# A hybrid two-layer trunk in fp32: one block of tokens runs ahead of the other between the layers, and layer B begins with two V products

## The chip, the cores and the metric

The kernel runs on one core of one Trainium2 chip. The core has a matrix engine (TensorE, "PE" in the profile; its weight loads are listed apart as "PEld"), a vector engine (VectorE, "DVE"), a scalar engine (ScalarE, "ACT"), GpSimd ("POOL") and a sync engine whose queue ("SP") issues the DMAs here. Weights and inputs are in HBM; tiles of 128 partitions are in SBUF; matmuls write into PSUM. The metric is the time of one execution on the device in microseconds, lower is better.

## The reference, cut to what matters

One sequence of 256 tokens, width 2048, goes through two layers: A (a Mamba-2 mixer) and B (dilated attention with shared K and V). Each layer ends with a residual, a gate and a LayerNorm over the 2048 features of a token.

```
def reference(x, c, ada_w, ada_b, ln_g, ln_b, a_in_w, ..., a_out_w, kv_w, b_in_w, b_out_w):
    for layer in range(2):
        shift, scale, gate = _adaln(c, ada_w[layer], ada_b[layer])     # silu(c) @ w + b
        h = x * (1.0 + scale) + shift
        if layer == 0:
            y = _ssd_mixer(h, ...)            # ends with y(256 x 4096) @ out_w(4096 x 2048)
        else:
            y = _dilated_mixer(h, k_sh, v_sh, b_in_w[0], b_out_w[0])
        x = _layer_norm(ALPHA * x + (1.0 + gate) * y, ln_g[layer], ln_b[layer])
        if layer == 0:
            k_sh, v_sh = split(x @ kv_w)      # kv_w: 2048 x 6144, K is the first half, V the second
    return x
```

K and V have three groups (g) of eight heads of 128 features. The kernel works on half a group at a time: `hq` is 0 or 1, and a half group is 512 columns.

## The kernel before, in words

**Tiling.** The 256 tokens are two blocks of 128 (`b` = 0, 1), the 2048 features sixteen tiles of 128 (`kt`). All matmuls are fp32 with split operands: every weight piece (128x1024 f32, 512 KB) is loaded by the SP queue into one of six `raw` buffers (`load_piece`, L85), ScalarE makes its rounded high half `whi` (L93), VectorE the low half `wlo` = raw - whi (L95). There are four buffers of each half. A product then has three matmuls per tile: high x high, high x low, low x high.

**Three forms of product.** `tm_mults` (L166) has the tokens as the stationary operand, 512 weight columns move, and the result is token-major; one piece (q) covers two feature tiles and has 6 matmuls for each block (L172 to L174). `cm_piece` (L109) has weights as the stationary operand and 256 tokens move; the result is feature-major (L119 to L121). `cm_wide` (L140) does the same for 256 columns with a 512-wide matmul over the high and low half of the tokens at once (L151) and a 256-wide one (L152), and adds the two sums (L156, L157). `tm_chunk` (L179) runs a whole token-major product; its last `split_end` pieces are held back, so that block 0's matmuls of them come first and then block 1's.

**Background work.** `queue` and `background` (L100, L253) spread the dot products of the next layer's scales, shifts and gates (L237, a 1 MB load and a 2048-wide VectorE operation each) over the pieces; `rate` (a, b) means a jobs per b pieces.

**The seam between the layers.** Layer A's output product is four `tm_chunk` calls over 512 columns (n = 0 to 3, L669), each followed for each block by `residual` (L648: gate, residual, statistics `bn_stats`). After the fourth, `ln_scale` (L654) makes mean and inverse deviation of both blocks in one chain of small VectorE operations, then u is normalised in five column ranges, block 0 on ScalarE (L687), block 1 on VectorE (L689). `x_tiles` (L698) transposes u into feature-major tiles on PE (L702), scales them into the high half `xhi` on ScalarE (L705), again in full precision into `xtmp` on VectorE (L706), and takes the difference as the low half `xlo` (L707). Layer B's first work is the three K products of hq = 0, whose pieces alternate (`cm_quads`, L123), with the x tiles of the next q made ahead of each. Behind them come the K products of hq = 1 (`cm_wide`), then the six V products (`tm_chunk`), with background jobs at a rate of (4, 9). While these run, GpSimd turns u into the residual of layer B (L759, L760).

**Order.** Each engine executes its instructions in order. The framework sets that order by the program's order as a priority and by what it takes to be ready; `tc.issue_after(ins)` puts the instructions of a block behind `ins` on its engine. Before, the low halves of the first weight pieces and all that follows the K products is put behind `nb_last`, the last operation of `ln_scale`.

**Memory.** Layer A's outputs y (eight tiles of 4 KB a partition) are in the pool `pa`, which is closed at the seam; the pool `pb` holds K and V in four tiles of 12 KB (`kk0`, `kk1`, `vt0`, `vt1`), two of them reused for the split gated output `oghi`, `oglo`, two for held weights of the last product.

Of the kernel before, what the change touches and what calls it, by code (L numbers as in the profile page):

```python
# [9 lines left out]
F32 = mybir.dt.float32  # L10
F32R = mybir.dt.float32r
# [12 lines left out]
G = 8  # L24
# [25 lines left out]
def trunk(ctx, tc, xT, x, c, par, cst, bias, lnrow, ada, wdt, win, wout, wkv, wk1, wbin, wbout, out):  # L50
# [72 lines left out]
    def cm_quads(work, ahi, alo, pre=None, after=None):  # L123
        for q in range(KT // 2):
            if pre:
                pre(q)
            for src, ps in work:
                cm_piece(src, q, ps, ahi, alo, after=after if q == 0 else None)

# [69 lines left out]
    sm.tile([P, 8], F32, name="pad", bufs=1)  # L199
# [72 lines left out]

    with ExitStack() as cA:
        pa = cA.enter_context(tc.tile_pool(name="pa", bufs=1))

        y = [pa.tile([P, 2, 512], F32, name=f"y{g}") for g in range(G)]
# [377 lines left out]
        def ln_scale(blocks=(0, 1)):  # L654
# [3 lines left out]
            for i, b in enumerate(blocks):  # L658
# [22 lines left out]
        drain()  # L681
        r, nb, nb_last = ln_scale()
        for c0_, c1_ in ((0, 256), (256, 512), (512, 1024), (1024, 1536), (1536, 2048)):
            for b in range(2):
                cs_ = slice(c0_, c1_)
                if b == 0:
                    S.activation(u[b][:, cs_], u[b][:, cs_], AF.Identity, bias=nb[:, b:b + 1], scale=r[:, b:b + 1])  # L687
                else:
                    V.tensor_scalar(u[b][:, cs_], u[b][:, cs_], r[:, b:b + 1], nb[:, b:b + 1],  # L689
                                    op0=ALU.mult, op1=ALU.add)  # L690
# [7 lines left out]
    def x_tiles(q):  # L698
        for kt in (2 * q, 2 * q + 1):
            pt = aux.tile([P, 512], F32, name="aux")[:, :L]  # L700
            for b in range(2):
                T.transpose(pt[:, b * P:b * P + P], u[b][:, kt * P:kt * P + P], ident)  # L702
            t = pl.tile([P, L], F32, name="xtmp")
            g_, b_ = pv("lng")[:, kt:kt + 1], pv("lnb")[:, kt:kt + 1]
            S.activation(xhi[:, kt, :], pt, AF.Identity, bias=b_, scale=g_)  # L705
            V.tensor_scalar(t, pt, g_, b_, op0=ALU.mult, op1=ALU.add)  # L706
            V.tensor_tensor(xlo[:, kt, :], t, xhi[:, kt, :].bitcast(F32), op=ALU.subtract)  # L707

    def ahead(q):

        if q == 0:
            x_tiles(0)
        if q < KT // 2 - 1:
            x_tiles(q + 1)

    kk = [pb.tile([P, 12, L], F32, name=f"kk{i}").rearrange("p (g i) l -> p g i l", g=NG) for i in range(2)]
    vt = [pb.tile([P, NG, 2, 512], F32, name=f"vt{i}") for i in range(2)]

    def evict_k(hq, g, ps):
        for w in range(2):  # L720
            S.activation(kk[hq][:, g, 2 * w:2 * w + 2, :], ps[w], AF.Copy)

    with ExitStack() as cL:
        pl = cL.enter_context(tc.tile_pool(name="pl", bufs=3))
        ex = cL.enter_context(tc.tile_pool(name="ex1", bufs=2, space=PSUM))
# [234 lines left out]
```

## Time and profile before

| what | value |
|---|---|
| median of three runs | 1301.03 us (1299.05 to 1304.12) |
| the profiled execution | 1303.79 us, span 1302.0 us |
| mean granted TensorE clock in it | 0.988 |
| HBM read | 332.41 MB |
| K products of hq = 0 (L119 first and last start) | 745.6 to 820.1 us |
| K products of hq = 1 (L151 first and last start) | 820.5 to 888.0 us |

How to read it: the span is the time from the first to the last instruction of the profiled execution, and its own time is a little longer. Busy times are sums over an engine's instructions; matmuls are pipelined, so the distance between starts, not the duration of one, is what a matmul costs in a stream. In the rows by stage, each engine has its busy time and the number of its instructions, then come the TensorE clock granted (1.00 is full), the mean busy share of the 16 DMA engines, and GB/s. The chain of waits is followed back from the last instruction; each line is start, time and what ran.

### The profile page before, as it was taken

What the parts mean: (1) busy time and instruction counts of PE and PEld (TensorE: products, weight loads), DVE (VectorE), ACT (ScalarE), POOL (GpSimd) and SP (SyncE); (2) the same over time, 40 slices, a digit from 0 to 9 for tenths busy, and PEclk for the clock granted to TensorE, in tenths of its full rate; (3) what the DMA queues carried; (4) which work ended last, traced back from release to release, by engine and by line L of the source; (5) the groups of instructions that cost most, each with busy time, mean ns of one, the idle gap of its engine ahead of it and who ended that gap; (6) DMA issues with size and microseconds to landing.
All of it is one profiled execution on the core that took longest, in us unless ns stands there. A gap on an engine that the chain in (4) does not pass through costs nothing.

```text
span 1302.0 us, 19326 instructions
## 1 busy us (share of the span) xinstructions
PE 1244.2 (96%) x7378; PEld 1096.7 (84%) x7378; DVE 1028.6 (79%) x1457; ACT 709.6 (55%) x1036; POOL 26.6 (2%) x20
## 2 busy tenths in 40 slices
PE   4999999999999999999999799999999999999995
PEld 3878988899898999878888699888887888888884
DVE  6689887899998778899775577988777757758677
ACT  3544457867587686864333444444435645444651
POOL 0000000000000000000000043000000000000000
PEclk9999999999999999999999899999999999999998
DMA  9999967696884556389977575999897864353561
GB/s 381 421 367 419 382 205 249 221 345 243 288 312 152 187 180 209 117 324 331 383 262 218 190 244 163 354 376 367 329 344 268 274 192 146 106 189 95 162 259 65
DMA packets 80445, 335.86 MB, mean 258 GB/s; under 512 B 8960, under 2 KB 9056, under 8 KB 67552
## 3 DMA queue, kind: packets, MB, share of 16 engines
q1 hardware_dynamic: 80352, 334.62, 71.7%
q8 instruction: 58, 0.95, 0.3%
q14 instruction: 35, 0.29, 0.1%
HBM read 332.41 MB, written 2.18 MB: 257 GB/s over the span
## 4 chain that ended last, share of the span: by engine, by line
PE 82%; DVE 9%; DMA 4%; ACT 3%; issue 2%; SPq 0%; DVEq 0%; ACTq 0%
PE acc L151 13%; PE acc L173 12%; PE acc L174 11%; PE acc L172 11%; PE acc L121 8%; PE acc L120 8%; PE acc L119 8%; PE acc L152 6%; DMA araw<-in_ada 4%; DVE araw L237 2%; DVE wlo L95 2%; PE py L579 1%; PE aux L788 1%; ACT whi L93 1%; DVE cacc L306 1%
## 5 line engine op out<-in xcount | busy, mean ns | idle before, releaser
L95 DVE TENSOR_TENSOR wlo<-raw,whi 128x1024 fp32r<-128x1024 f32 x395 | 484.9, 1240 | 191.4 <-ACT whi L93 189.9
L93 ACT ACTIVATE whi<-raw 128x1024 fp32r<-128x1024 f32 x395 | 412.8, 1056 | 334.8 <-PE acc L174 140.8
L119 PE MATMUL acc<-actT,whi 128*128 128x256 f32 x960 | 274.1, 288 | 23.4 <-ACT whi L93 19.3
L173 PE MATMUL acc<-wlo,actT 128*128 128x512 f32 x704 | 277.2, 394 | 3.2 <-DVE wlo L95 3.1
L121 PE MATMUL acc<-actT,wlo 128*128 128x256 f32 x960 | 272.3, 288 | 4.5 <-DVE wlo L95 4.4
L120 PE MATMUL acc<-actT,whi 128*128 128x256 f32 x960 | 273.8, 286 | 0.6 <-DVE actT L384 0.6
L172 PE MATMUL acc<-whi,actT 128*128 128x512 f32 x704 | 272.9, 395 | 0.8 <-ACT actT L634 0.7
L151 PE MATMUL acc<-actT,whi 128*128 128x512 f32 x704 | 250.9, 398 | 0.0
L237 DVE SCALAR_TENSOR_TENSOR araw<-araw,cb__72 128x2048 f32<-128x2048 f32 x96 | 219.4, 2286 | 17.0 <-DMA araw<-in_ada 16.5
L119 PEld LDWEIGHTS acc<-actT,whi 128*128 128x128 f32 x960 | 186.8, 196 | 25.3 <-ACT whi L93 20.4
L152 PE MATMUL acc<-actT,wlo 128*128 128x256 f32 x704 | 201.4, 286 | 0.0
L121 PEld LDWEIGHTS acc<-actT,wlo 128*128 128x128 f32 x960 | 185.9, 195 | 7.1 <-DVE wlo L95 7.0
L120 PEld LDWEIGHTS acc<-actT,whi 128*128 128x128 f32 x960 | 187.7, 196 | 1.0 <-DVE actT L384 0.8
L174 PE MATMUL acc<-whi,actT 128*128 128x512 f32 x448 | 175.5, 392 | 0.0
L173 PEld LDWEIGHTS acc<-wlo,actT 128*128 128x128 f32 x704 | 132.7, 188 | 33.4 <-DVE wlo L95 6.9
L151 PEld LDWEIGHTS acc<-actT,whi 128*128 128x128 f32 x704 | 132.3, 188 | 30.2
L172 PEld LDWEIGHTS acc<-whi,actT 128*128 128x128 f32 x704 | 132.2, 188 | 28.7 <-ACT actT L634 1.5
L152 PEld LDWEIGHTS acc<-actT,wlo 128*128 128x128 f32 x704 | 133.2, 189 | 0.5
L174 PE MATMUL acc<-whi,ylo 128*128 128x512 f32 x256 | 100.3, 393 | 0.0
L174 PEld LDWEIGHTS acc<-whi,actT 128*128 128x128 f32 x448 | 84.4, 188 | 17.2
L174 PEld LDWEIGHTS acc<-whi,ylo 128*128 128x128 f32 x256 | 48.0, 188 | 9.7
L306 DVE SCALAR_TENSOR_TENSOR cacc<-acc,prm,cacc 128x253 f32<-128x253 f32 (+2 forms) x96 | 42.0, 474 | 6.6 <-ACT cacc L303 6.4
(204 smaller groups left out, 1077.8 us busy)
## 6 DMA issues: line engine op xcount, KB each, us to landing
araw<-in_ada SPq DMA_DIRECT2D x96, 1024.0 KB, 7.4
raw<-in_win SPq DMA_DIRECT2D x160, 512.0 KB, 5.4
raw<-in_wkv SPq DMA_DIRECT2D x72, 512.0 KB, 6.1
raw<-in_wout SPq DMA_DIRECT2D x64, 512.0 KB, 5.2
raw<-in_wbin SPq DMA_DIRECT2D x64, 512.0 KB, 3.6
raw<-in_wk SPq DMA_DIRECT2D x24, 512.0 KB, 7.8
cbc<-cumd SPq DMA_DIRECT2D x16, 512.0 KB, 5.2
raw<-in_wbout SPq DMA_DIRECT2D x16, 512.0 KB, 3.7
```

The lines of the kernel that those rows point to most:

```text
L93: S.activation(hi, raw, AF.Copy)
L95: latest[0] = V.tensor_tensor(lo, raw, hi.bitcast(F32), op=ALU.subtract)
L119: T.matmul(o, hi[:, k, c_], ahi[:, kt, :], start=first, stop=False, skip_group_check=True)
L120: T.matmul(o, hi[:, k, c_], alo[:, kt, :], start=False, stop=False, skip_group_check=True)
L121: T.matmul(o, lo[:, k, c_], ahi[:, kt, :], start=False, stop=kt == k1 - 1, skip_group_check=True)
L151: T.matmul(ps[n], hi[:, k, c_], xp[:, kt], start=kt == 0, stop=False, skip_group_check=True)
L152: T.matmul(ps[n][:, 0, :], lo[:, k, c_], xhi[:, kt, :], start=False, stop=kt == KT - 1, skip_group_check=True)
L172: T.matmul(ps[b], h_, hi[:, k, :], start=kt == k0, stop=False)
L173: T.matmul(ps[b], h_, lo[:, k, :], start=False, stop=False)
L174: T.matmul(ps[b], l_, hi[:, k, :], start=False, stop=kt == k1 - 1)
L237: V.scalar_tensor_tensor(raw, raw, 1.0, cb_, op0=ALU.mult, op1=ALU.mult, accum_out=mod[layer][:, ct, j:j + 1])
L306: V.scalar_tensor_tensor(acc[:, o:], ps[:, :L - o], w[:, j:j + 1], acc[:, o:], op0=ALU.mult, op1=ALU.add)
```

## The change: block 0 goes ahead, and V comes first

- The last product of layer A's output holds four pieces back instead of two. After it, each block has its own residual, its own `ln_scale((b,))` and its own normalisation of the first 512 columns; the rest is normalised later.
- During that product (q = 2, 5, 8, 11) the first four weight pieces of two V products (q = 0 and 1 of `wv[0]` and `wv[2]`) are loaded and split, into tiles that held y (`first_weights`). y now lies in a pool `slots` that stays open; its eight tiles then hold weights, K and V, the gated output and held weights.
- Layer B begins with these two V products. For each block: four x tiles of that block alone, the rest of its normalisation, then the matmuls of the four early pieces for that block; x tiles 4 and 5 come in the middle of block 1's. Then q = 2 to 7 alternate between the two products, with two x tiles ahead of each q.
- Behind them: the third V product of hq = 0, all six K half groups by `cm_wide`, the three V products of hq = 1. The form with weights stationary and 256 tokens moving (`cm_quads`) is no longer used here.
- The splits of q = 2 and all that follows the first two products are put behind `tile4`, the last operation of block 1's fourth x tile.
- The background jobs of layer A's products have rate (1, 2) in the second and third product and are drained after the third.

```diff
-    sm.tile([P, 8], F32, name="pad", bufs=1)
+    sm.tile([P, 16], F32, name="pad", bufs=1)
...
+    slots = ctx.enter_context(tc.tile_pool(name="slots", bufs=1))
...
-        y = [pa.tile([P, 2, 512], F32, name=f"y{g}") for g in range(G)]
+        y = [slots.tile([P, 2, 512], F32, name=f"s{g}") for g in range(G)]
...
+        first_v, norm = [], []
+
+        def normalise(b, c0_, c1_):
+            (r, nb, _), cs_ = norm[b], slice(c0_, c1_)
+            if b == 0:
+                S.activation(u[b][:, cs_], u[b][:, cs_], AF.Identity, bias=nb, scale=r)
+            else:
+                V.tensor_scalar(u[b][:, cs_], u[b][:, cs_], r, nb, op0=ALU.mult, op1=ALU.add)
+
+        def first_weights(q):
+
+            if q % 3 == 2 and q < 12:
+                i = q // 3
+                into = [slots.tile([P, 1024], F32R, name=f"s{2 * i + j}") for j in range(2)]
+                first_v.append(split(load_piece(wv[2 * (i % 2)][i // 2]), into=into))
+
         for n in range(4):
             ps = tm_chunk(wout[n], lambda kt: yhi[kt // 16][:, kt % 16, :], lambda kt: ylo[kt // 4][:, kt % 4, :],
-                          nk=2 * KT, rate=(1, 3) if n else (0, 1), pre=None if n else y_ahead,
-                          split_end=2 if n == 3 else 0)
+                          nk=2 * KT, rate=(1, 2) if n in (1, 2) else (0, 1),
+                          pre={0: y_ahead, 3: first_weights}.get(n), split_end=4 if n == 3 else 0)
             if n == 0:
                 queue(pn, cols1[:16])
+            if n == 2:
+                drain()
...
                 residual(n, ps[b], b, (gt, u[b][:, 512 * n:512 * n + 512]), xr)
-        drain()
-        r, nb, nb_last = ln_scale()
-        for c0_, c1_ in ((0, 256), (256, 512), (512, 1024), (1024, 1536), (1536, 2048)):
-            for b in range(2):
...
+                if n == 3:
+                    norm.append(ln_scale((b,)))
+                    normalise(b, 0, 256)
+                    normalise(b, 256, 512)
...
+    def x_tile(kt, blocks=(0, 1)):
+        c_ = slice(P * blocks[0], P * blocks[-1] + P)
+        pt = aux.tile([P, 512], F32, name="aux")[:, :L]
+        for b in blocks:
+            T.transpose(pt[:, b * P:b * P + P], u[b][:, kt * P:kt * P + P], ident)
+        t = pl.tile([P, L], F32, name="xtmp")
+        g_, b_ = pv("lng")[:, kt:kt + 1], pv("lnb")[:, kt:kt + 1]
+        S.activation(xhi[:, kt, c_], pt[:, c_], AF.Identity, bias=b_, scale=g_)
+        V.tensor_scalar(t[:, c_], pt[:, c_], g_, b_, op0=ALU.mult, op1=ALU.add)
+        return V.tensor_tensor(xlo[:, kt, c_], t[:, c_], xhi[:, kt, c_].bitcast(F32), op=ALU.subtract)
...
-        ps = [acc_pair(), acc_pair(), acc_pair(ex)]
-        cm_quads([(wkv[2 * g], ps[g]) for g in range(NG)], xhi, xlo, pre=ahead, after=nb_last.ins)
-        for g in range(NG):
-            evict_k(0, g, ps[g])
+
+        vps = [tm_pair(), tm_pair()]
+        for b in range(2):
+            for kt in range(4):
+                tile4 = x_tile(kt, (b,))
+            for n in range(1, 4):
+                normalise(b, 512 * n, 512 * n + 512)
+            for i, w in enumerate(first_v):
+                if b and i == 2:
+                    x_tile(4)
+                    x_tile(5)
+                tm_mults(i // 2, w, vps[i % 2], hx, lx, 0, KT, (b,))
+        for q in range(2, KT // 2):
+            if q < KT // 2 - 1:
+                x_tile(2 * q + 2)
+                x_tile(2 * q + 3)
+            for j in range(2):
+                w = split(load_piece(wv[2 * j][q]), after=tile4.ins if q == 2 else None)
+                tm_mults(q, w, vps[j], hx, lx, 0, KT, range(2))
+        for g in range(2):
+            evict_v(0, g, vps[g])
 
         R = (4, 9)
         pin[0] = latest[0].ins
-        with tc.issue_after(nb_last.ins):
+        with tc.issue_after(tile4.ins):
             queue(pl, cols1[16:])
             jobs.append(lambda: gate_out(1))
-            for g in range(NG):
-                for w in range(2):
-                    cm_wide(wk1[2 * g + w], kk[1][:, g, 2 * w:2 * w + 2, :], rate=R)
+            evict_v(0, 2, tm_chunk(wv[4], hx, lx, rate=R))
             for hq in range(2):
                 for g in range(NG):
-                    ps = tm_chunk(wkv[6 + 2 * g + hq], hx, lx, rate=R)
-                    for b in range(2):
-                        S.activation(vt[hq][:, g, b, :], ps[b], AF.Copy)
+                    kv[hq, g] = place(3 + 3 * hq + g, [P, 4, L])
+                    for w in range(2):
+                        cm_wide(wk[2 * (2 * g + hq) + w], kv[hq, g][:, 2 * w:2 * w + 2, :], rate=R)
+            for g in range(NG):
+                evict_v(1, g, tm_chunk(wv[1 + 2 * g], hx, lx, rate=R))
             drain()
...
-    oghi = pb.tile([P, H, L], F32R, name="kk0")
-    oglo = pb.tile([P, H, L], F32R, name="vt0")
...
+    oghi, oglo = ([slots.tile([P, 4, L], F32R, name=f"s{2 * hq + i}") for hq in range(2)] for i in range(2))
...
-    spare = {"hi": pb.tile([P, 3, 1024], F32R, name="kk1"), "lo": pb.tile([P, 3, 1024], F32R, name="vt1")}
     held = []
     for i in range(8):
-        into = [spare[h][:, i, :] if i < 3 else pf.tile([P, 1024], F32R, name=f"{h}{i}") for h in ("hi", "lo")] \
-            if i < 7 else None
+        j = 4 + 2 * i
+        into = [slots.tile([P, 1024], F32R, name=f"s{j + k}") if j < 8 else
+                pb.tile([P, 1024], F32R, name=f"b{j + k}") if j < 12 else
+                pf.tile([P, 1024], F32R, name=f"f{j + k}") for k in range(2)] if i < 7 else None
         held.append(split(load_piece(wbout[2 + i // 4][i % 4]), into=into))
```

Here `place(i, shape)` gives the tile `s{i}` of `slots` for i under 8 and `b{i}` of `pb` above, and `evict_v(hq, g, ps)` copies the two blocks of a V product from PSUM into its place with ScalarE (places 0 to 2 for hq = 0, 9 to 11 for hq = 1).

More of the change, by code (lines that the diff above doesn't have):

```diff
@@ L696, in trunk @@
     hx, lx = (lambda kt: xhi[:, kt, :]), (lambda kt: xlo[:, kt, :])
-    def x_tiles(q):
-        for kt in (2 * q, 2 * q + 1):
-            pt = aux.tile([P, 512], F32, name="aux")[:, :L]
-            for b in range(2):
[L702 to L707, printed above, removed]
@@ L723, in trunk, with place, evict_v @@
+    kv, vt = {}, {}
+    def place(i, shape):
+        return slots.tile(shape, F32, name=f"s{i}") if i < 8 else pb.tile(shape, F32, name=f"b{i}")
+    def evict_v(hq, g, ps):
+        vt[hq, g] = place(3 * hq + g if hq == 0 else 9 + g, [P, 2, 512])
+        for b in range(2):
+            S.activation(vt[hq, g][:, b, :], ps[b], AF.Copy)
     with ExitStack() as cL:
         pl = cL.enter_context(tc.tile_pool(name="pl", bufs=3))
-        ex = cL.enter_context(tc.tile_pool(name="ex1", bufs=2, space=PSUM))
@@ L726, in trunk @@
[L726 to L729 removed]
+        vps = [tm_pair(), tm_pair()]
+        for b in range(2):
+            for kt in range(4):
[7 more added lines that the diff above has]
+                tm_mults(i // 2, w, vps[i % 2], hx, lx, 0, KT, (b,))
@@ L787, in attend @@
                     pq = aux.tile([P, 512], F32, name="aux")[:, :n]
-                    T.matmul(pq, qq[:, g, i, b * P:b * P + P], kk[hq][:, g, i, :n], start=True, stop=True)
+                    T.matmul(pq, qq[:, g, i, b * P:b * P + P], kv[hq, g][:, i, :n], start=True, stop=True)
                     bi = pc2.tile([P, 256], F32, name="bi", bufs=2)[:, :n]
```

39 lines of the change are left out of this document (7 added, 32 removed).

## The prediction

> **What bounds the kernel now.** The page first: who is busy, and which engine the chain of waits runs through.
>
> ```profile
> span 1302.0 us, 19326 instructions
> PE 1244.2 (96%) x7378; PEld 1096.7 (84%) x7378; DVE 1028.6 (79%) x1457; ACT 709.6 (55%) x1036; POOL 26.6 (2%) x20
> PE 82%; DVE 9%; DMA 4%; ACT 3%; issue 2%; SPq 0%; DVEq 0%; ACTq 0%
> ```
>
> TensorE (PE) is the bound, so a change can pay in three ways: fewer or cheaper matmuls, less idle PE, or less time at a lowered clock. Next the busy times by stage: two of the four products of layer A's output (the second and the fourth), then the seam between the layers in three pieces.
>
> ```profile
> core 0: us, PE busy (x) PEld busy (x) DVE busy (x) ACT busy (x) POOL busy (x), PEclk, DMA share, GB/s
> ...
> 606.00:649.50 43.50, 43.50 (x194) 36.02 (x193) 35.49 (x36) 17.00 (x16) 0.00 (x0) 1.00 0.99 374
> ...
> 693.00:736.80 43.80, 43.79 (x194) 35.92 (x192) 21.59 (x23) 16.98 (x16) 0.00 (x0) 1.00 0.62 189
> 736.80:745.60 8.80, 1.40 (x5) 0.60 (x5) 8.22 (x24) 4.79 (x8) 0.00 (x0) 0.76 0.72 263
> 745.60:752.00 6.40, 6.40 (x31) 6.40 (x32) 5.81 (x11) 1.41 (x3) 0.09 (x1) 0.52 0.81 232
> 752.00:820.40 68.40, 68.40 (x575) 68.40 (x575) 51.56 (x51) 32.44 (x40) 26.34 (x16) 1.00 0.66 212
> ```
>
> PE is full on both sides of 736.80 to 745.60; there it works 1.4 of 8.8 us, and the 6.4 us behind it run at a granted clock of 0.52. The chain of waits says what stands in the hole:
>
> ```profile
> 736.56 0.24 PE acc L174
> 736.83 0.70 DVE u L650
> ...
> 739.01 0.27 DVE m01mv L659
> ...
> 741.67 0.17 DVE m01nb L664
> 741.87 3.21 ACT u L687 x5
> 745.08 0.46 ACT actT L705
> 745.58 1.65 PE acc L119 x6
> ...
> 757.62 0.44 PE aux L702 x4
> 766.69 0.44 PE aux L702 x4
> ```
>
> After the last matmul of layer A (736.80) come block 1's residual on DVE (2.2 us to 739.01), the serial statistics (2.8 us to 741.84), five ScalarE (ACT) normalisations in a row (3.2 us), the first transposed tile, and only then matmuls. From there one round of three K pieces with its four transposes repeats every 9.07 us.
>
> **The size of the hole.** The end of the K stage is the first wide product (L151):
>
> ```profile
> L151 PE MATMUL acc<-actT,whi x192: 395/398/403, 820.5 to 888.0; 128*128 128x512 f32 x192
> ```
>
> From 736.8 to 820.5 are 83.7 us; eight rounds at 9.07 are 72.6. So the seam costs **11.1 us**: this is all there is to win there. It holds the idle PE and 6.4 us at about half clock (3.1 us).
>
> **Term 1: other forms of product.** The pitch of the split weights gives the time of a token-major piece (both blocks, 12 matmuls):
>
> ```profile
> 724.32 1.23 DVE L95 TENSOR_TENSOR wlo<-raw,whi 128x1024 fp32r<-128x1024 f32 x1 [1.49 <-ACT whi L93]
> 727.04 1.23 DVE L95 TENSOR_TENSOR wlo<-raw,whi 128x1024 fp32r<-128x1024 f32 x1 [1.50 <-ACT whi L93]
> ```
>
> 2.72 us, so 21.8 for 512 columns of V, in both kernels six times. A wide K product (256 columns) has 32 of the 192 pairs above: 67.5 us over 191 pairs is 0.353 a pair, 11.3 a product. The three K products of before cost 8 x (9.07 - 0.44) = 69.0 together. Before: 69.0 + 6 x 11.3; after: 12 x 11.3. The term is 67.8 - 69.0 = **-1.2 us**. Transposes: as many as before.
>
> **Term 2: the seam after the change.** Let t = 0 be the end of block 0's matmuls in layer A's last product. With four pieces held back, block 1's half still runs until t = 5.44 (four times 2.72/2). Under it goes block 0's residual and statistics: from the chain, 741.87 - 736.80 = 5.1 us to the first normalisation, about 0.6 us for that (3.21 us for five), then transposes (0.44 for four) and a first high half (0.46 for a whole tile). First matmul of layer B at about t = 6.6: **(a) 1.2 us idle**.
>
> The third matmul needs the low half, which is made on DVE, and DVE starts block 1's residual at t = 5.5 and its statistics at 7.7 (done at 10.5 if nothing comes between). Does DVE let tiles of block 0 in between? Another serial statistics chain, in layer A, shows that it does:
>
> ```profile
> 554.45 0.17 DVE L584 TENSOR_SCALAR ms<-ss 128x2 f32<-128x2 f32 x1 [0.41 <-ACT py L582]
> ...
> 556.13 1.22 DVE L95 TENSOR_TENSOR wlo<-raw,whi 128x1024 fp32r<-128x1024 f32 x1
> ...
> 560.55 0.15 DVE L213 SCALAR_TENSOR_TENSOR ay<-at,ay 128x2 f32<-128x2 f32 x1
> ```
>
> Whatever is ready goes between the steps, and that chain took 6.1 us. I take it so: first low half at about t = 8 and **(b) 1.0 us** of waiting beyond the two matmuls that need no low half. The price is that block 1's chain gets longer by block 0's eight small operations. Rows for those:
>
> ```profile
> L95 DVE TENSOR_TENSOR wlo<-raw,whi 128x1024 fp32r<-128x1024 f32 x24 | 36.3, 1526 | 15.2 <-ACT whi L93 15.2
> L707 DVE TENSOR_TENSOR actT<-xtmp,actT 128x256 fp32r<-128x256 f32 x16 | 9.9, 660 | 0.0
> L706 DVE TENSOR_SCALAR xtmp<-aux,prm 128x256 f32<-128x256 f32 x16 | 7.9, 536 | 0.6 <-ACT actT L705 0.6
> ...
> L208 DVE TENSOR_TENSOR m01y<-magic,m01s 128x2 int32<-128x2 int32 x1 | 0.2, 161 | 0.0
> ```
>
> A half tile (128x128) isn't in the trace: it lies between 0.16 (128x2) and 0.54 us (128x256); I take the middle, 0.35, so 2.8 us for eight. Block 1's statistics then end at about t = 13.3, and its first matmul can start at about 14.5. The Trainium skill, page "VectorE: DVE Perf Modes", section "The TRN2 errata", speaks against halved tiles: each instruction carries a fixed cost, and fp32 tensor_tensor takes (N+151)/0.96 ns. An estimate from that page is 0.29 us for 128 elements against 0.42 for 256, so two halves cost 0.16 more than a whole; for the sixteen operations of the eight half tiles that would be some 1.3 us of DVE time, and the sum by it stays within 0.5 us of mine.
>
> Block 0's 24 matmuls take 5.44 us at full clock. Whether the clock holds is the next question. One other short hole in the trace:
>
> ```profile
> 390.00:392.00 2.00, 1.07 (x5) 0.56 (x3) 2.00 (x3) 0.00 (x0) 0.00 (x0) 1.00 0.87 350
> 392.00:394.00 2.00, 0.94 (x5) 0.94 (x6) 2.00 (x4) 1.27 (x3) 0.00 (x0) 0.82 0.07 27
> 394.00:396.00 2.00, 2.00 (x7) 1.52 (x6) 2.00 (x4) 1.18 (x3) 0.00 (x0) 0.50 0.00 0
> 396.00:398.00 2.00, 2.00 (x9) 1.64 (x8) 2.00 (x6) 0.00 (x0) 0.00 (x0) 0.83 0.00 0
> ```
>
> About 2 us of idle PE (0.93 + 1.06) was enough to lower the clock: lost are 0.36 + 1.0 + 0.34 = 1.7 us. (a) and (b) add up to 2.2, so I charge **(c) 1.7 us** once. Block 0's matmuls then end at 6.6 + 5.44 + 1.0 + 1.7 = 14.7, and block 1's are ready at 14.5: no second hole. The page "TensorE: Matmul & The Clock Gate" of the Trainium skill, in the table of "Why this matters for your kernels", allows gaps up to about 3 us before the clock falls. Here the trace differs (2 us sufficed), so it decides; by the page (c) is 0, but a second hole of 1.5 us takes its place, and the sum moves by 0.2.
>
> Then the two V products. A round of two pieces and two tiles is 5.44 + 0.44 = 5.9 us of PE. DVE has, at the means above, 2 x 1.53 + 2 x (0.66 + 0.54) = 5.5 us. These means are stretched from 1.23 (quoted above) to 1.53 while POOL works on u (26.3 us in the 68.4 us stage). It keeps up, barely; after tile4 it is behind with the splits that were told to wait for it (`after=tile4.ins`) and with everything queued behind those: I charge **(d) 0.7 us**, bounds 0 to 7.
>
> New seam: 1.2 + 1.0 + 1.7 + 0.7 = 4.6 us, against 11.1.
>
> **Edits costed at nothing.** Four early weight splits in the fourth product: ACT 4 x 1.06 on 16.98 of 43.8 us, DVE 4 x 1.23 on 21.59, and four loads of 0.5 MB on SP's queue on 189 GB/s, where 374 was reached in the second product. Without that cover the four splits would be 4.9 us on DVE in the seam. The faster rate (1,2) moves two or three 1 MB loads per product to where the DMA share is already 0.99: at 374 GB/s that is 7.5 us of transfer. PE idles nowhere in that row, and six raw buffers are 16 us ahead, so I take 0, bounds 0 to +3. The background jobs behind the seam keep their 4 per 9 pieces: 80 pieces give room for 35, and there are 33. New pools, places and the held weights of the last product change which buffer waits for which, all on tiles read long before.
>
> **Sum.** -1.2 + 4.6 - 11.1 = **-7.7 us**. The profiled execution took 1303.79 us (span 1302.0), which becomes 1296.1; it lay 2.8 above the median of the runs, 1301.03, which becomes **1293.3 us** (-0.6%).
>
> **Rivals.**
> - B, DVE and the clock don't get in the way: only (a) and 0.5 of (d) are left, 1.7 us: -10.6, 1290.4. For it: DVE mixes chains freely. Against: the lowered clock at 392.
> - C, block 0's low halves stand behind block 1's whole chain: the first comes at t = 10.5 + 0.4 (block 1's first normalisation, between the same bounds) + 0.7 = 11.6. Idle 11.6 - 5.44 - 0.45 = 5.7, half clock 3.1 as now, 0.5 behind it: 9.3, so -3.0, 1298.0. For it: block 1's operations come first in the program. Against: the filled chain at 554.
> - D, slower: DVE becomes the bound. The two splits of q = 3, which no edge holds back (1.23 each), enter block 1's chain as at 556, and the first low half comes at 14.1: 8.2 idle + 3.1. Then POOL's 26.3 us fall into 44 us of V products instead of 68, and the 24 x 0.3 = 7.1 us of stretching doubles, which DVE no longer has to spare: 18.4 in the seam, +6.1, 1307.1. It turns slower from a seam of 12.3 us on. For it: 5.5 of 5.9 us. Against: PE is full in the row from 752 on.
> - E, the change doesn't do what it says: the order on the engines leaves both statistics ahead of every tile, and the 11.1 us move with the end of block 1. Only term 1 stays: -1.2, 1299.8.
>
> **How the numbers follow.** Forecast 0.52, B 0.13, C 0.10, D 0.20, E 0.05. A measurement of this kernel tells about 0.5% (6.5 us) from no change. Below 1294.5: 0.45 of the forecast and B, 0.58. Above 1307.5: 0.15 of D. Between: 0.07 + 0.10 + 0.05 + 0.05 = 0.27. The forecast's own range is 1291 to 1296; the range from B to the near side of D is 1289.5 to 1303.5.
>
> **What would show it.** In the changed profile: block 0's first transposes within 1.5 us of the end of layer A's last matmul (a); block 0's low halves between steps of block 1's statistics on DVE (b), not behind them (C); granted clock under 1.0 for some 4 us, no longer (c); no PE wait for wlo or actT over 1 us in the V products (d, else D); wide products of 11.3 us, twelve of them. It is wrong if PE waits more than 6 us in all between the layers, or if a stall appears in the second or third output product.

## The result, and the profile after

The changed kernel took 1307.38 us (median of 11 runs, 1302.16 to 1312.73), the kernel before 1301.24 us beside it (11 runs, 1297.82 to 1306.72): ratio 1.0044, 95% interval 1.0025 to 1.0064. That is slower by 6 us, or 0.44%: little, but the interval lies above 1. Forecast were 1293.3, with a range up to 1303.5. The profiled execution took 1307.17 us, its span is 1305.4 (before 1302.0).

First the page of the kernel after: span, busy times, and the shares of the chain of waits.

```profile
span 1305.4 us, 18995 instructions
PE 1245.4 (95%) x7186; PEld 1085.9 (83%) x7186; DVE 1038.4 (80%) x1490; ACT 709.1 (54%) x1046; POOL 26.5 (2%) x20
PE 83%; DVE 9%; DMA 3%; ACT 3%; issue 2%; SPq 0%; DVEq 0%; ACTq 0%
```

PE has 192 matmuls fewer and is busy for as long as before. Cutting the span at the starts of the same work in each kernel shows where the time went (us; from the timelines: the first gate operation of each output product's residual, the last of the fourth's, the first wide K product, the first query product, the end):

| kernel | to product 1's end | 2nd | 3rd | 4th | seam and first products | rest of K, V | last part | span |
|---|---|---|---|---|---|---|---|---|
| before | 606.6 | 42.7 | 43.5 | 44.0 | 83.7 | 200.2 | 281.3 | 1302.0 |
| after | 605.2 | 51.0 | 43.7 | 43.9 | 76.1 | 203.4 | 282.1 | 1305.4 |
| e1 slow rate | 604.5 | 42.6 | 43.8 | 43.7 | 76.2 | 201.4 | 282.7 | 1294.9 |
| e2 fast rate alone | 601.9 | 50.6 | 43.3 | 44.0 | 82.9 | 199.7 | 282.1 | 1304.5 |
| e3 no scaling on GpSimd | 603.6 | 51.9 | 43.5 | 44.0 | 71.7 | 203.4 | 281.1 | 1299.2 |
| e4 tiles first | 604.0 | 55.2 | 43.5 | 44.0 | 74.3 | 203.4 | 282.0 | 1306.3 |
| e5 = e1 + e4 | 600.5 | 42.7 | 43.9 | 43.7 | 74.2 | 201.4 | 281.9 | 1288.3 |
| e7 fast rate, later start | 599.8 | 43.5 | 45.2 | 42.3 | 76.1 | 201.0 | 281.1 | 1289.0 |
| e13 half dots, half loads | 607.8 | 42.8 | 43.6 | 44.0 | 74.5 | 205.2 | 282.0 | 1299.9 |

The stage of the seam gave 7.5 us. By the forecast's prices 3.6 of these come from its products: three V products (65.4 us) stand there now, three K products (69.0) stood there before. The K and V products behind it took back 3.2 (2.4 of them planned: six wide products of 11.3 more, three token-major ones of 21.8 fewer). The second output product lost 8.3. The part up to product 1 ends anywhere from 599.8 to 607.8 us, in kernels that differ little there, so single spans can't be compared as a whole; medians can, and stages with the caveat that each comes from one execution.

Now the windows of the kernel after: in each row from, to, length, the busy times of PE, PEld, DVE, ACT and POOL, the granted clock, the DMA share, GB/s.

```profile
606.00:649.50 43.50, 39.61 (x162) 31.92 (x161) 38.47 (x36) 13.76 (x13) 0.00 (x0) 0.92 0.90 335
...
610.00:614.00 4.00, 1.75 (x8) 1.13 (x6) 4.00 (x4) 1.06 (x1) 0.00 (x0) 1.00 0.88 298
614.00:618.00 4.00, 2.35 (x6) 1.88 (x7) 4.00 (x6) 0.00 (x0) 0.00 (x0) 0.61 1.00 389
618.00:622.00 4.00, 4.00 (x12) 3.12 (x11) 3.80 (x4) 1.06 (x1) 0.00 (x0) 0.54 0.86 322
...
743.50:745.00 1.50, 0.78 (x4) 0.36 (x4) 1.25 (x2) 1.50 (x4) 0.00 (x0) 1.00 0.00 0
745.00:747.00 2.00, 1.72 (x7) 0.87 (x7) 1.97 (x9) 2.00 (x4) 0.00 (x0) 1.00 0.38 61
...
758.70:762.00 3.30, 0.91 (x5) 0.49 (x5) 3.30 (x5) 0.26 (x1) 0.97 (x1) 0.95 0.38 53
762.00:765.00 3.00, 3.00 (x9) 2.42 (x9) 3.00 (x6) 0.87 (x2) 2.67 (x2) 0.50 1.00 294
```

Two holes in PE, each with a lowered clock behind it: at 610 to 616 in the second product, which was full before, and at 759 to 761, inside the first V products. The short holes of the seam itself (743.5 to 747) leave the clock at 1.00. VectorE's timeline (start, time, line, operation, tile, shape, count) tells the first one:

```profile
599.54 1.22 DVE L95 TENSOR_TENSOR wlo<-raw,whi 128x1024 fp32r<-128x1024 f32 x1
600.67 2.29 DVE L230 SCALAR_TENSOR_TENSOR araw<-araw,cb__72 128x2048 f32<-128x2048 f32 x1
...
602.88 2.29 DVE L230 SCALAR_TENSOR_TENSOR araw<-araw,cb__72 128x2048 f32<-128x2048 f32 x1
...
605.83 1.22 DVE L95 TENSOR_TENSOR wlo<-raw,whi 128x1024 fp32r<-128x1024 f32 x1
...
609.36 2.28 DVE L230 SCALAR_TENSOR_TENSOR araw<-araw,cb__72 128x2048 f32<-128x2048 f32 x1
...
612.17 2.27 DVE L230 SCALAR_TENSOR_TENSOR araw<-araw,cb__72 128x2048 f32<-128x2048 f32 x1
...
614.37 4.62 DVE L95 TENSOR_TENSOR wlo<-raw,whi 128x1024 fp32r<-128x1024 f32 x4
```

Between the splits of 599.54 and 614.37 lie four dots (4 x 2.3), the six residual operations of the first product (6 x 0.68) and one split: 14.8 us without a gap. PE uses one low half every 2.72 us, and there are four buffers, a store of 10.9 us. One split more makes 13.6. The store runs dry, and PE's timeline has the wait, with its releaser in brackets. The four splits at 614.37 run without a gap, so their high halves were ready: it was not a late load that held PE up here. The rows below the first one are the seam:

```profile
615.65 0.80 PE L166 MATMUL acc<-wlo,actT 128*128 128x512 f32 x1 [3.89 <-DVE wlo L95]
...
743.29 0.39 PE L167 MATMUL acc<-whi,ylo 128*128 128x512 f32 x1
743.96 0.44 PE L710 MATMUL aux<-cc,u 128*128 128x128 f32 x2 [0.28 <-ACT u L670]
744.84 0.50 PE L165 MATMUL acc<-s,actT 128*128 128x512 f32 x1 [0.44 <-ACT actT L713]
...
746.92 0.50 PE L167 MATMUL acc<-s,actT 128*128 128x512 f32 x1
...
751.40 0.39 PE L167 MATMUL acc<-s,actT 128*128 128x512 f32 x1
751.63 0.38 PE L710 MATMUL aux<-cc,u 128*128 128x128 f32 x2
752.45 0.50 PE L165 MATMUL acc<-s,actT 128*128 128x512 f32 x1 [0.44 <-ACT actT L713]
...
761.26 1.14 PE L710 MATMUL aux<-cc,u 128*128 128x128 f32 x4 [2.37 <-DVE xtmp L714]
```

And VectorE in the seam, where block 0's half tiles (128x128) stand between the steps of block 1's statistics (m11):

```profile
745.17 0.69 DVE L648 BATCH_NORM_STATS2 st<-u 128x6 f32<-128x512 f32 x1
745.78 0.39 DVE L714 TENSOR_SCALAR xtmp<-aux,prm 128x128 f32<-128x128 f32 x1
746.09 0.25 DVE L655 BATCH_NORM_AGGREGATE m11mv<-st 128x2 f32<-128x24 f32 x1
...
746.58 0.28 DVE L715 TENSOR_TENSOR actT<-xtmp,actT 128x128 fp32r<-128x128 f32 x1
...
749.65 0.16 DVE L660 SCALAR_TENSOR_TENSOR m11nb<-m11mv,m11y 128x1 f32<-128x1 f32 x1
...
756.23 4.52 DVE L95 TENSOR_TENSOR wlo<-raw,whi 128x1024 fp32r<-128x1024 f32 x2
760.67 0.98 DVE L714 TENSOR_SCALAR xtmp<-aux,prm 128x256 f32<-128x256 f32 x2
```

The hole at 759 is in the last two rows: the two splits of q = 2, put behind `tile4`, run before `xtmp` of x tiles 4 and 5. They took 2.26 us each, not 1.23, as GpSimd scaled u at the same time (its row below). Loads alone didn't stretch a split: the four at 614.37 took 1.16 each with the DMA share at 1.00. PE, in order, stands at the next transposes, which need a PSUM tile back from `xtmp`, and the matmuls queue behind them.

```profile
756.11 3.55 POOL L781 TENSOR_TENSOR u<-u,lnr 128x512 f32<-128x512 f32 x2
```

### The profile page after: what moved, and what is told of

The parts are those of the page before. It is cut to its first block, busy times and chain, and to the rows that moved or that the text cites. A ratio compares the mean times of both kernels' runs of the same rounds, so it can differ in the third digit from the quotient of the medians.

```text
span 1305.4 us, 18995 instructions
## 1 busy us (share of the span) xinstructions
PE 1245.4 (95%) x7186; PEld 1085.9 (83%) x7186; DVE 1038.4 (80%) x1490; ACT 709.1 (54%) x1046; POOL 26.5 (2%) x20
## 4 chain that ended last, share of the span: by engine, by line
PE 83%; DVE 9%; DMA 3%; ACT 3%; issue 2%; SPq 0%; DVEq 0%; ACTq 0%
PE acc L144 16%; PE acc L166 12%; PE acc L167 12%; PE acc L165 11%; PE acc L145 8%; PE acc L121 6%; PE acc L120 6%; PE acc L119 6%; DMA araw<-in_ada 3%; DVE araw L230 2%; DVE wlo L95 2%; PE py L575 2%; PE aux L809 1%; ACT whi L93 1%; PE po L823 1%
## 5 line engine op out<-in xcount | busy, mean ns | idle before, releaser
L95 DVE TENSOR_TENSOR wlo<-raw,whi 128x1024 fp32r<-128x1024 f32 x391 | 478.2, 1236 | 163.2 <-ACT whi L93 161.5
L93 ACT ACTIVATE whi<-raw 128x1024 fp32r<-128x1024 f32 x391 | 406.7, 1055 | 295.1 <-PE acc L167 126.3
L144 PE MATMUL acc<-actT,whi 128*128 128x512 f32 x896 | 318.0, 399 | 0.0
L166 PE MATMUL acc<-wlo,actT 128*128 128x512 f32 x688 | 272.5, 396 | 6.5 <-DVE wlo L95 6.4
L165 PE MATMUL acc<-whi,actT 128*128 128x512 f32 x688 | 269.8, 398 | 0.8 <-ACT actT L630 0.7
L119 PE MATMUL acc<-actT,whi 128*128 128x256 f32 x768 | 218.6, 287 | 21.8 <-ACT whi L93 19.3
L120 PE MATMUL acc<-actT,whi 128*128 128x256 f32 x768 | 218.7, 286 | 0.6 <-DVE actT L380 0.6
L144 PEld LDWEIGHTS acc<-actT,whi 128*128 128x128 f32 x896 | 167.6, 188 | 38.6
L167 PE MATMUL acc<-whi,actT 128*128 128x512 f32 x432 | 169.2, 392 | 0.0
L119 PEld LDWEIGHTS acc<-actT,whi 128*128 128x128 f32 x768 | 149.0, 194 | 23.3 <-ACT whi L93 20.4
L165 PEld LDWEIGHTS acc<-whi,actT 128*128 128x128 f32 x688 | 130.2, 190 | 27.8 <-ACT actT L630 1.5
L120 PEld LDWEIGHTS acc<-actT,whi 128*128 128x128 f32 x768 | 149.7, 195 | 1.0 <-DVE actT L380 0.8
L167 PEld LDWEIGHTS acc<-whi,actT 128*128 128x128 f32 x432 | 81.4, 188 | 16.8
```

The source lines that it names most:

```text
L93: S.activation(hi, raw, AF.Copy)
L95: latest[0] = V.tensor_tensor(lo, raw, hi.bitcast(F32), op=ALU.subtract)
L119: T.matmul(o, hi[:, k, c_], ahi[:, kt, :], start=first, stop=False, skip_group_check=True)
L120: T.matmul(o, hi[:, k, c_], alo[:, kt, :], start=False, stop=False, skip_group_check=True)
L144: T.matmul(ps[n], hi[:, k, c_], xp[:, kt], start=kt == 0, stop=False, skip_group_check=True)
L165: T.matmul(ps[b], h_, hi[:, k, :], start=kt == k0, stop=False)
```

## The experiments

Theory one: the loss is the faster rate, the seam works about as forecast. Rival: the seam itself lost. **The rate, put back and alone.** e1 is the kernel after with

```diff
-                          nk=2 * KT, rate=(1, 2) if n in (1, 2) else (0, 1),
+                          nk=2 * KT, rate=(1, 3) if n in (1, 2) else (0, 1),
```

> The changed kernel with the background rate of layer A's second and third output product back at one job per three pieces; all else as changed. Theory (the faster rate puts two 2.3 us dot products ahead of weight splits at the start of the second output product; PE stands 3.9 us and then runs at a lowered clock for some 6 us): this stall goes, the second product takes 43.5 us again, and the time falls by 6 to 7 us from the changed kernel's 1307.4, to about 1300.8, that is a ratio to before of 0.995 to 1.000. Rival (the stall comes from the new places of y and the weights): the second product still takes about 50 us and the time stays at 1306 to 1308.

e2 is the kernel before with the changed rate and a `drain()` after n = 2 (the one after n = 3 then finds nothing left):

```diff
-                          nk=2 * KT, rate=(1, 3) if n else (0, 1), pre=None if n else y_ahead,
+                          nk=2 * KT, rate=(1, 2) if n in (1, 2) else (0, 1), pre=None if n else y_ahead,
...
+            if n == 2:
+                drain()
```

> The kernel before with nothing changed but the rate (one job per two pieces in the second and third output product, none in the fourth, drained after the third). Theory: the same stall appears without any of the rest, +6 to +7 us, about 1307.8, with a PE wait for wlo of 3 to 4 us between 606 and 650. Rival (the rate hurts only together with the new places or the early weights): no such wait, 1300 to 1302.

e1 took 1294.0 us (ratio 0.9955, 0.9939 to 0.9972), e2 1306.61 (1.0051, 1.0032 to 1.0069), with a wait for wlo of 5.9 us. The same window of the second product in e1, then in e2:

```profile
606.00:649.50 43.50, 43.50 (x193) 35.95 (x193) 35.55 (x36) 16.99 (x16) 0.00 (x0) 1.00 0.99 377
```

```profile
606.00:649.50 43.50, 37.63 (x160) 30.62 (x159) 36.38 (x33) 13.26 (x13) 0.00 (x0) 0.92 0.92 342
```

The stall comes and goes with the rate, in the old kernel as in the new. Without it the rest of the change is worth 0.45%, and the time is 0.7 us from the forecast. From the kernel after to e1 the time fell by 13.4 us, twice what was expected (11.6 by the ratios to the kernel before); the second product accounts for 8.4 and the K and V products for 2.0, and the rest isn't assigned. VectorE is as busy in e1 as in the kernel after: 19.64 and 19.66 us of the 20 from 596 to 616. What differs is the stretch between two splits, 7.1 us in e1 where it was 14.8:

```profile
600.97 1.22 DVE L95 TENSOR_TENSOR wlo<-raw,whi 128x1024 fp32r<-128x1024 f32 x1
...
608.05 4.61 DVE L95 TENSOR_TENSOR wlo<-raw,whi 128x1024 fp32r<-128x1024 f32 x4
```

**Density or start?** e7 lets the first job of the second product wait for six pieces and keeps the rate; e14 has the fast rate in the third product only.

```diff
+            if n == 1:
+                state[0] = -4
```

> The changed kernel with the fast rate kept, but the first job only after six pieces of the second output product, instead of two. Theory (the stall is made at the start of that product, where two dot products and the residual's six operations stand ahead of the splits): the wait for wlo there falls under 1 us and the time to 1295 to 1299. Rival (it is the density, one 1 MB load and one 2.3 us operation per two pieces, wherever it begins): the stall only moves, 1304 to 1308.

```diff
-                          nk=2 * KT, rate=(1, 2) if n in (1, 2) else (0, 1),
+                          nk=2 * KT, rate={1: (1, 3), 2: (1, 2)}.get(n, (0, 1)),
```

> The kernel after with the slow rate (1,3) in the second output product and the fast rate (1,2) only in the third. Theory 'the loss comes at the start of the second product, where the dots of this layer's own gate, the residual and the first dots of the next layer meet': no wait over 1 us in either product, both 42.5 to 44 us, time 1291 to 1296. Rival 'the fast rate costs wherever it stands': the third product 46 to 50 us, time 1298 to 1304.

e7 took 1291.96 us (0.993, 0.9918 to 0.9941), below its band, e14 1294.8 (0.9946, 0.9927 to 0.9965), inside it; in both PE is full at clock 1.00 from 606 to 693. So the fast rate did no harm later in the second product or in the third; what it costs depends on where it starts. At the start of the second product VectorE was full already; this is the kernel before:

```profile
596.00:616.00 20.00, 20.00 (x91) 16.51 (x90) 19.70 (x24) 8.40 (x10) 0.00 (x0) 1.00 0.92 335
```

19.70 of 20 us: the last y tiles, the first residual and the dots meet here. PE lived on the store of low halves.

**Time on VectorE or loads?** e8 multiplies only half of each vector (1024 of 2048 inputs, for the first sixteen) and loads all of it; e11 loads half and multiplies that half twice; e13 halves both. Here e8:

```diff
-            V.scalar_tensor_tensor(raw, raw, 1.0, cb_, op0=ALU.mult, op1=ALU.mult,
+            m = D // 2 if layer == 1 and kind != "gate" and ct < 8 else D
+            V.scalar_tensor_tensor(raw[:, :m], raw[:, :m], 1.0, cb_[:, :m], op0=ALU.mult, op1=ALU.mult,
```

> The changed kernel with the fast rate, where the sixteen dot products of layer A's output products go over the first 1024 of their 2048 inputs: the loads are the same, the VectorE operation is half as long (the second half of these sums is left out). Theory (VectorE's order makes the stall): the wait for wlo in the second product falls under 1 us, 1299 to 1302. Rival (the loads make it, at a DMA share near 1): PE still waits 3 us or more there, for wlo or for a load behind it, 1305 to 1308.

```diff
+        if layer == 1 and kind != "gate" and ct < 8:
+            nc.sync.dma_start(raw[:, :D // 2], ada[layer, KIND.index(kind), ct][:, :D // 2])
+        else:
+            nc.sync.dma_start(raw, ada[layer, KIND.index(kind), ct])
...
+            for _ in range(D // m):
```

> The kernel after, but of the first sixteen background vectors of layer B only half (1024 of 2048 inputs, 0.5 MB) is loaded, while each dot still keeps VectorE for about as long as before, as two operations over the same half (it leaves out the other half of these sums). It is the counterpart of the kernel with half dots and full loads (1300.5, wait for wlo in the second output product 1.4 us). Theory 'the time of the dots on VectorE makes the stall': wait for wlo 3 us or more, second product 48 to 51 us, time 1302 to 1307. Rival 'the extra loads make it, by a busier DMA or by standing ahead of the weight pieces on the queue': wait below 1.5 us, second product 43 to 46 us, time 1292 to 1299.

> The kernel after, but of the first sixteen background vectors of layer B only half (1024 of 2048 inputs) is loaded and only that half is multiplied, in one operation (it leaves out the other half of these sums). Half the dots with full loads took 1300.5, half the loads with the whole time on VectorE 1299.6. Theory 'both the time on VectorE and the loads ahead of the weight pieces carry the loss, and only together they are it': second output product 42.5 to 44 us, no wait for wlo or whi over 1 us in it, time 1292 to 1296 like the slow rate. Rival 'the jobs cost by their number and place, whatever their size': product 47 to 49 us, time 1298 to 1301.

e8 took 1300.48 us (0.9993, 0.9978 to 1.0008), inside its band, with a second product of 47.9 us. Its waits are 1.4 us for wlo (under 1 was expected) and, ahead of that, 0.6 for whi, and here a load is behind them. SP's timeline of e8 has seven vector loads in a row ahead of the next weight pieces, and ScalarE's waits from 598 to 660 (in all, times, longest) have one of 9.0 us for such a piece:

```profile
579.20 22.24 SPq L223 DMA_DIRECT2D araw<-in_ada  x7
601.54 0.86 SPq L87 DMA_DIRECT2D raw<-in_wout  x2
```

```profile
ACT whi L93 <- DMA raw<-in_wout: 13.0, 6, 9.0
```

So e8 halves the time on VectorE but also has another order of loads, and its stall isn't simply what is left of the first one. e11 took 1299.57 (0.9988, 0.9976 to 1.0001): a time between its two bands, but waits for wlo of 3.2 us in four and a second product of 48.2, as the theory of VectorE's time had it. It divides each dot into two shorter operations as well, so it doesn't tell how much is due to the loads. e13 took 1297.26 (0.9969, 0.9952 to 0.9985), without a wait in the product, 42.8 us long:

```profile
606.00:649.50 43.50, 43.50 (x193) 36.04 (x192) 25.82 (x29) 16.98 (x16) 0.00 (x0) 1.00 0.76 235
```

So the number and place of the jobs don't cost by themselves; their size does: with both halved the stall is gone, with only one of them halved the second product stays over 5 us longer than with the slow rate. That e13's time lies above its band comes from elsewhere, as far as its profile shows: its K and V products have 3.1 us of waits for VectorE and ScalarE, and take 3.8 longer than e1's:

```profile
PE acc L145 <- DVE wlo L95: 2.7, 3, 1.0
...
PE acc L144 <- ACT whi L93: 0.4, 1, 0.4
```

**An order by force.** e9 keeps the fast rate and puts each dot behind the newest split ahead of it in the program:

```diff
+            if near[0]:
+                pin[0] = latest[0].ins
             jobs.pop(0)()
...
+                near[0] = True
```

> The kernel after, with the faster rate kept, but each background dot of layer A's output products put behind the newest weight split that the program has before it on VectorE, so that no dot can run ahead of the splits that precede it. Theory 'the framework moves the large dots of 2.3 us ahead of splits that come earlier in the program, and the splits are then late': the wait for wlo in the second output product (3.9 us in the kernel after) goes below 1 us, that product takes 42 to 45 us instead of 51, clock 0.98 or more in it, and the time falls to 1291 to 1299, near that of the kernel with the rate put back (1294.0). Rival 'the rate itself is too dense for the start of the product, in any order': the wait stays at 2 us or more, the product at 48 us or more, the time at 1302 to 1308.

It took 1330.03 us (1.0228, 1.0204 to 1.0253): neither band. Its second product took 67.6 us. ScalarE's waits from 598 to 700, and SP's timeline:

```profile
ACT whi L93 <- DMA raw<-in_wout: 35.1, 8, 8.1
```

```profile
633.04 2.77 SPq L226 DMA_DIRECT2D araw<-in_ada  x2
635.90 0.38 SPq L87 DMA_DIRECT2D raw<-in_wout  x1
640.62 2.83 SPq L226 DMA_DIRECT2D araw<-in_ada  x2
643.54 0.38 SPq L87 DMA_DIRECT2D raw<-in_wout  x1
```

A dot that runs later gives its buffer back later; the load of the next vector waits for that buffer on the SP queue (41.8 us in all from 598 to 670), and the weight pieces stand behind it, one every 7.6 us where PE needs one every 2.72. The first two dots still ran together ahead of a split, so the question whether another order alone would have cured the stall isn't answered.

**The hole at 759.** e3 leaves out GpSimd's scaling of u and its loads; e4 puts the splits of q = 2 behind x tile 5:

```diff
-            for b in range(2):
-                PO.tensor_tensor(u[b][:, cs_], u[b][:, cs_], lnr[0], op=ALU.mult)
-                PO.tensor_tensor(u[b][:, cs_], u[b][:, cs_], lnr[1], op=ALU.add)
...
```

> The changed kernel without the LayerNorm weights and biases on layer B's residual (the sixteen GpSimd operations on u and their eight loads are left out). Theory (POOL stretches the VectorE splits behind the fourth x tile, so x tiles 6 and 7 come late): the PE wait of 2.4 us for an x tile at 758.7 falls under 0.8 us and the time by 3 to 4 us, to about 1304. Rival (the order on VectorE, two weight splits ahead of x tiles 4 and 5, makes that wait by itself): the wait shrinks only by the stretching of those two splits, 1 us at most stays away, and the time falls by 1 us or less.

```diff
-                    x_tile(5)
+                    tile5 = x_tile(5)
...
-                w = split(load_piece(wv[2 * j][q]), after=tile4.ins if q == 2 else None)
+                w = split(load_piece(wv[2 * j][q]), after=tile5.ins if q == 2 else None)
```

> The changed kernel with the splits of q = 2 behind x tile 5 (the sixth) instead of behind block 1's fourth x tile. Theory of the order: PE no longer waits 2.4 us for a free transpose buffer, a wait for wlo of about 1 us may take its place, the clock stays up, and the time falls by 2 to 4 us, to 1303.5 to 1305.5. Rival (VectorE with POOL is the bound there, whatever the order): the same wait appears as a wait for wlo, and the time stays within 1 us of 1307.4.

e3 took 1300.57 us (1.0003, 0.9989 to 1.0018), e4 1302.68 (1.0021, 1.0004 to 1.0038), both lower than either of their bands. PE's waits from 700 to 1010, in e3 and in e4, and e3's two splits:

```profile
PE aux L710 <- DVE xtmp L714: 0.2, 1, 0.2
```

```profile
PE acc L166 <- DVE wlo L95: 1.5, 2, 1.2
...
PE aux L710 <- DVE xtmp L714: 0.2, 1, 0.2
```

```profile
754.41 2.35 DVE L95 TENSOR_TENSOR wlo<-raw,whi 128x1024 fp32r<-128x1024 f32 x2
```

Taking the scaling away cures the wait: the two splits take 1.18 us each, still ahead of the x tiles, and the seam stage falls from 76.1 to 71.7 us. So the order alone didn't make the wait. Changing the order cures it too, but now the splits are late: 1.5 us of it come back as waits for low halves, and the stage takes 74.3. The stall of the second product is in both. In the profiled execution of e4, the slowest of its twelve, that stall was larger, 12.5 us.

**Together.** e5 is e1 with e4's edit, e10 is e7 with e4's edit, e12 is e1 with e3's:

> The changed kernel with the old rate in the second and third output product (as in e1) and the splits of q = 2 behind x tile 5 (as in e4). e1 took 0.9955 of before, e4 took 0.0023 off the changed kernel. Theory (the two stalls are independent): about 0.993 of before, 1291 to 1293, and no PE wait over 1 us for an x tile behind the seam. Rival (VectorE is the bound in the V products, so the wait comes back as one for wlo or whi): 0.995 to 0.996, as e1.

> The kernel after with two edits that worked alone: the first background job of the second output product only after six pieces (alone 1291.96), and the splits of the two V products' third pieces put behind the x tiles 4 and 5 instead of in front of them (alone 1302.7 against 1307.4 of the kernel after). Theory 'the two stalls are independent': the gains add up: second product 42 to 44 us, no wait for an x tile over 1 us, time 1286 to 1290, ratio to the kernel before 0.988 to 0.991. Rival 'the second gain depends on the first, because the wait for an x tile moves to a wait for a split': 1290.5 to 1293, ratio 0.9915 to 0.9935, no better than either alone.

> The kernel after with the slow rate put back (alone 1294.0) and without GpSimd's scaling of u and its loads (alone 1300.6 against 1307.4; it leaves out the second layer's scaled residual). Theory 'the two costs lie in different places and add up': seam loss 2 to 4 us instead of 7.4, waits for x tiles below 0.5 us, time 1287 to 1290, near the time at which vector engine and clock do not get in the way (1290.4). Rival 'the seam is bound by the order on VectorE even without the stretching': loss 6 us or more, time 1292 to 1294.

e5 took 1290.43 us (0.9917, 0.9904 to 0.993): the lowest median, 10.9 us below the kernel before. e10 took 1292.26 (0.9929, 0.9908 to 0.9949), no better than e7 alone, as its rival had it (its stage is 74.3 instead of 76.1, a gain within the scatter of the whole). e12 took 1291.3 (0.9936, 0.9912 to 0.9959), 1.3 above its band, with a seam stage of 71.7 us and a span of 1287.2: the stages add up, the medians, over 7 us of spread, only roughly.

**Moving the scaling away.** e6 is e1 with the scaling in slices of 128 columns during the attention, into one buffer each:

```diff
+    for n in range(KT):
+        cs_ = slice(P * n, P * n + P)
+        lnr = [pc2.tile([P, P], F32, name=f"lnr{i}", bufs=1) for i in range(2)]
+        for i in range(2):
+            bcast(lnr[i], lnrow, i * D + P * n)
...
```

> The changed kernel with the old rate (as in e1) and the scaling of layer B's residual moved behind the K and V products: its weights and biases are loaded in slices of 128 columns into the memory that is free only then, so GpSimd works during the attention. Theory (GpSimd's stretching of VectorE is most of the stall behind the seam; e3 took 5 us off by leaving it out): 3 to 5 us less than e1, 1289 to 1291, 0.991 to 0.993 of before. Rival (in the attention the same stretching costs as much): 1293 to 1297, no better than e1.

It took 1315.8 us (1.0107, 1.009 to 1.0124). The seam stage was 71.7 us as hoped; the part after the query products' start took 306 us instead of 283 in e1. SP's timeline of e6, then a window of PE there:

```profile
1052.51 3.46 SPq L63 DMA_DIRECT2D lnr<-in_lnrow  x2
1056.02 0.42 SPq L87 DMA_DIRECT2D raw<-in_wbin  x1
1057.03 3.50 SPq L63 DMA_DIRECT2D lnr<-in_lnrow  x2
1060.59 0.93 SPq L87 DMA_DIRECT2D raw<-in_wbin  x1
```

```profile
1060.00:1100.00 40.00, 29.56 (x126) 22.59 (x125) 11.30 (x13) 10.62 (x14) 14.13 (x33) 0.86 0.49 151
```

The loads of the slices wait for their single buffer ahead of the weight pieces, which come one in 4.6 us. It is the same fault as in e9: a load whose buffer isn't free yet holds up what is behind it on the queue.

## Why the prediction was wrong

- **The step that failed is "Edits costed at nothing": the faster rate, taken as 0 with bounds 0 to +3.** It cost 8.3 us in the second product (e2, without anything else of the change: 7.9). The step argued with a store that wasn't the scarce one: six raw buffers. What PE lives on are four low halves, 10.9 us, and VectorE makes them; at the start of the product 14.8 us of other work stood there with one split in it. The row quoted there had VectorE at 35.49 of 43.5 us; three dots more, at 2.3, make 42.4. Taken finer, at 596 to 616, it had 0.3 us to spare. The prediction looked at the loads and at PE, and not at the engine on which the added instruction runs. Its last sentence had named the sign: a stall in the second output product. Open is whether the same dots in another order would have stalled PE.
- **(a) and (b) were right, block 1's start by luck.** 1.3 us pass until the first matmul (743.52 to 744.84, the first two transposes among it; forecast 1.2). The first low half starts at 746.58, 8.5 us after block 0's last matmul (forecast 8; rival C 11.6), between steps of block 1's statistics; PE waits about 1.0 us for it. An operation on block 0's half tiles took 0.28 to 0.41 us (0.35 was taken). Block 1's first matmul comes 14.4 us after the same point (forecast 14.5), but not on the path forecast: its statistics ended at 11.7 us, not 13.3, and block 0's matmuls at 13.6, not 14.7, as the clock held. Block 1's transposes stood behind these on PE, and 0.4 us of waiting came on top.
- **(c) 1.7 us didn't come there.** The clock stays at 1.00 through these holes of 1.3 and 1.0 us. It fell behind the 2.37 us hole at 759 instead, to 0.50 for 3 us: 1.5 us lost.
- **(d) 0.7 us was mis-sized.** At block 1's first matmul and behind it there are a wait of 0.4, one of 2.4 and the clock's 1.5: 4.3 us, inside the bounds of 0 to 7. The step saw the splits pinned behind `tile4`, but charged them at their mean; beside GpSimd they took 2.26 us, and x tiles 4 and 5 stood behind them. Without the scaling the stage is 4.4 us shorter (e3), with the other order 1.9 (e4). With 68.8 us of matmuls and transposes in the stage, the seam cost 7.4 us against 4.6 forecast; the items named here make 6.6 of it, and the rest isn't assigned. The Trainium skill, page "GPSIMD Engine Reference", section "8. Key points", says that GpSimd shares its SBUF interfaces with VectorE and contends with VectorE instructions that have two SBUF inputs. A split has two, and the trace agrees: 1.22 us alone, 2.26 beside it.
- **Term 1** held: 201.4 us for the rest of K and V in e1 against 200.2 before, 1.2 more where 12 wide and three token-major products at the forecast prices give 2.4 more. The kernel after has 2.0 us of waits for wlo in them. So have e3 and e4, and e8, e11 and e13 have 2.7; e1, e5, e7 and e14 have none. Why isn't shown: e7 has the fast rate too, and e13 has no stall in the second product.
- **The rivals.** D's 1307.1 is the time measured, by chance: of its mechanism only the stretching beside GpSimd is there, and its seam of 18.4 us isn't. B, C and E fell: VectorE does get in the way, low halves are not held back, block 0 does run ahead.

With the failed step taken out (e1), the change is worth 6.6 us where 7.7 were forecast. That it comes so near is in part luck: the seam cost 2.8 us more than forecast, the K and V products behind it 1.2 less.

## What to carry to other kernels

An added background operation is priced on the engine that runs it, in the narrowest window that it falls into: how many products of that engine lie in store, how long they last, and how much of that time is taken already. An average busy share of 80% said nothing about a stretch of 15 us. Here a load that waited for its buffer delayed everything behind it on the load queue (e6, e9); a rearrangement that looks local is best first read along that queue.

## What was not expected of the hardware

A hole of 2.37 us in PE (0.91 us busy of 3.3) brought the granted clock to 0.50 for about 3 us, one of 3.89 to 0.61 and 0.54 in the windows from 614 to 622, while two holes of about 1 us within 3.5 us left it at 1.00, and so did four waits of 0.6 to 1.3 us in e11's second product. In e8, waits of 0.6 and 1.4 us two microseconds apart brought it to 0.71 (610 to 614). From what length on a hole does this, these runs don't tell. Of the 8.3 us of the second product the clock took nearly as much as the wait, by an estimate from the row of 606 to 649.5: 0.08 of 43.5 us, 3.5, beside 3.9. The Trainium skill, page "TensorE: Matmul & The Clock Gate", section "Why this matters for your kernels", wants no gap over about 3 us; in this trace 2.4 was enough.
